# A two-column read of a shared PSUM bank, moved from a score block's fourth matmul to its fifteenth

## The chip, the cores and the metric
The program runs on one core of one Trainium2 chip. The metric is the device time of one execution in microseconds (us). Before the change the median of three runs is 3346.76 us (3344.51 to 3351.8).

## What the program computes
One transformer block over 1024 tokens of width 2048, plus 256 context tokens. Cut to the part that the change touches, the reference is a differential attention: every one of 8 heads has two maps, and their softmax weights are subtracted.

```
hx = modulate(rmsnorm(x), ...);  q, k, v, p, gb, gc, xin = split(hx @ w_in)      # k, v also from the context
s  = einsum('bqhmd,bkhmd->bhmqk', q, k) * 64 ** -0.5      # m = 0, 1: the two maps, 64 wide each
a  = softmax(s);  w = a[:, :, 0] - lam * a[:, :, 1];  o = w @ v
x  = x + gate * (concat(rmsnorm(o), pool_mix(p), conv_mix(gb, gc, xin)) @ w_out)
x  = x + gate2 * expert_choice_ffn(...);  return rmsnorm(x)
```

The whole is done in float32, where a product of two matrices is made of three matmuls on rounded high and low parts (high with high, high with low, low with high).

## The kernel before, in words
The program has four stages: modulation and projections for the first 768 tokens, the attention (with the projections of the other 256 tokens and a part of the output projection beside it), the rest of the output projection with norm and router, and the 16 experts.

The attention runs 64 steps: a head, a block of 256 queries, and one half of it (128 queries). Each step computes the scores of its 128 queries against 1280 keys for both maps. Python writes the steps one behind the other in a loop (functions `score`, `combine`, `turn`, `value`): the scores of the step two ahead, VectorE's combination of the next one's two exponentials, ten transposes of the combined weights in three groups (with casts to high and low parts by ACT and VectorE, tiles wth and wtl), and, for every second step, 30 matmuls of the weights with the values (tile av). Between them `fill` puts in a counted share of the projection matmuls (tile gm), whose weights ACT casts (line 439) and POOL completes (line 440). Small blocks for pooling and convolution run beside this (lines 847 to 904): a load of a tile pl_x or cv_z on SP's queue, a bias add on ACT (line 861, writes pl_x) or a scaling on ACT (line 896, writes e_out), and then POOL or VectorE.

What order the engines finally work in is not Python's alone. The tile scheduler takes this order, works out which instruction needs which other one, and writes a list for each engine by its own model of when an instruction is ready. Each engine then works through its own list in order.

One score block (`score`, line 952) is 18 matmuls into one PSUM tile sc of 128 by 2560, map 0 in the first 1280 columns and map 1 behind it. PSUM is divided into banks of 512 columns of this type. Map 0 uses rows 0 to 63 of TensorE and map 1 rows 64 to 127, so that a matmul of each may run side by side. Each map's keys are cut into three chunks (table CH), each chunk takes three matmuls, and PAIRED sorts the 18 so that the maps alternate:

```
CH = (((1024, 1280), (0, 512), (512, 1024)), ((256, 768), (768, 1280), (0, 256)))
```

Map 0's first chunk fills columns 1024 to 1279, which is the first half of the third bank. Map 1's last chunk fills columns 1280 to 1535, the second half of the same bank. The two must not be written by both maps at once, and a copy on ACT of two columns (to a tile named turned, which nothing reads) orders them: it reads what map 0's first chunk wrote, and the next matmul on the tile waits for it. In sorted order, the matmuls 1, 3 and 4 are map 0's first chunk, and 15, 17 and 18 are map 1's last one. Behind the block VectorE takes the negated maximum of each map (line 970, tile nm), and ACT the exponential with its sum (line 975, tile e). There is one tile sc, so a block can start only when the second exponential of the block before it has read it.

Of the kernel before, what the change touches and what calls it, by code (L numbers as in the profile page):

```python
# [9 lines left out]
F32 = mybir.dt.float32  # L10
# [10 lines left out]
P = 128  # L21
# [135 lines left out]
def nosync(tc, later, earlier):  # L157
    if earlier is not None:
        tc.add_manual_dep(later.ins, earlier.ins.name,
                          mybir.DependencyInfo(mybir.DependencyClass.NoSync, mybir.DependencyReason.DATA),  # L160
                          reason="accumulation groups of one bank in order")


def block_kernel(tc, I, out, dbg=None):
    nc = tc.nc
    pe, act, dve, gp, sp = nc.tensor, nc.scalar, nc.vector, nc.gpsimd, nc.sync
# [3 lines left out]
    def mm(o, l, r, start=True, stop=True):  # L170
        return pe.matmul(o, l, r, start=start, stop=stop, skip_group_check=True)  # L171
# [403 lines left out]
    def run_chunk(*args, beside=None):  # L575
        c = ChunkA(*args)
        for k in range(KT):
            if beside:
                next(beside, None)
            c.step(k)  # L580
        run_later()
        return c
# [67 lines left out]
    for h in range(HEADS):  # L650
        c = run_chunk(OFF_Q + h * P)
# [7 lines left out]
    for g in range(4):  # L659
        c = run_chunk(OFF_GC + g * P)  # L660
# [4 lines left out]
        c = run_chunk(OFF_X + g * P)  # L665
# [24 lines left out]
    sc = psc.tile([P, 2 * NKEY], F32, name="sc")  # L690
# [6 lines left out]
    asm = mk("asm", bufs=2, side="right")  # L697
# [257 lines left out]
    def score(i):  # L955
        h, b, qt = steps[i]
        q = Q_[h, b]
        k = K_[visit[i]]
        for _, m, c, n in PAIRED:
            c0, c1 = CH[m][c]  # L960
            rows = slice(64 * m, 64 * m + 64)
            one = mm(sc[:, m * NKEY + c0:m * NKEY + c1], q[rows, n // 2, qt * P:(qt + 1) * P], k[rows, n % 2, c0:c1],
               start=(n == 0), stop=(n == 2))
            if (m, c, n) == (0, 0, 2):
                act.copy(asm.tile([P, 2], F32, name="turned", tag="turned"), sc[:, c0:c0 + 2])
        scored.append(one)
        for m in range(2):
            s = sc[:, m * NKEY:(m + 1) * NKEY]
            nm = asm.tile([P, 1], F32, name="nm", tag=f"nm{m}")
            r = dve.tensor_reduce(nm, s, axis=AX, op=ALU.max, negate=True)  # L970
            if T["nsy"]:
                nosync(tc, r, last_stt[0])
            e = ep.tile([P, NKEY], F32, name=f"e{m}", tag=f"e{m}", bufs=(LEAD + 1, 2)[m])
            ssum = s0C[:, b, h, qt:qt + 1] if m == 0 else asm.tile([P, 1], F32, name="s1", tag="s1")
            act.activation(e, s, AF.Exp, bias=nm, scale=1.0, accum_out=ssum)  # L975
            E_[i, m] = (e, ssum)
# [195 lines left out]
    if True:  # L1172
# [14 lines left out]
        for i in range(LEAD):  # L1187
            score(i)
            fill(T["f3"])
# [3 lines left out]
        for i in range(NS):  # L1193
# [16 lines left out]
            for op in T[("late" if late else "even") if qt == 0 else ("lato" if late else "odd")]:  # L1210
                if isinstance(op, float):
                    part(op)
                elif op == "S" and nxt:
                    score(nxt)
                elif op == "V":
                    if waiting is not None:
                        value(waiting)
                        if visit[waiting] != visit[i]:
                            load_v(visit[i], 1)
                        waiting = None  # L1220
                    if i + 2 < NS and visit[i + 2] != visit[i]:
                        load_v(visit[i + 2], 0)
                elif op[0] == "T":
                    turn(i, int(op[1]))
                elif op == "C" and i + 1 < NS:
                    combine(i + 1)
# [436 lines left out]
```

## Time and profile before

| what | value |
|---|---|
| median of three runs | 3346.76 us |
| the profiled execution | 3349.19 us |
| its span, from the first to the last instruction | 3347.4 us |
| TensorE matmuls busy | 3070.2 us, 92% of the span |
| VectorE, ACT, POOL busy | 2258.2, 1768.6, 879.7 us |
| reads of sc into turned | 64, 10.7 us in all |

All rows are from one profiled execution. Times are counted from the start of its span. PE is TensorE's matmuls and PEld its weight loads, which overlap the matmuls; DVE is VectorE, POOL is GpSimd, SP the engine that issues most loads. L171 is the helper through which nearly every matmul is recorded, so matmuls are told apart by their tiles: `sc<-ks,qs` is a score matmul, `gm` a projection, `av` a value matmul, `trw` a transpose of weights. An arrow in brackets names what ended an engine's idle time. A row of the timeline with x4 merges four equal or like instructions that follow each other, with the time from the first's start to the last's end.

### The profile page before, as it was taken

To read this page: it belongs to the slowest core of one execution; us is meant where nothing else is said; L and a number is where in the kernel's file an instruction comes from. 1 tells how busy PE (TensorE), PEld (TensorE's weight loads), DVE (VectorE), ACT (ScalarE), POOL (GpSimd) and SP (SyncE) were. 2 spreads that over 40 slices of the span, in tenths; PEclk is the share of its full clock that TensorE was granted. 3 is DMA by queue.
4 is the path that set the end of the run, shared out by engine and by line. 5 is a ranking of instruction groups with operands and counts; after the bars stand their busy time and mean duration, and the time that the engine had idled before them with its cause. 6 is when DMAs were issued, how large, how long until landed. Compare 5 with 4: busy or idle time off the path is not lost. (4 is left out here: it accounts for less than half of the span.)

```text
span 3347.4 us, 48671 instructions
## 1 busy us (share of the span) xinstructions
PE 3070.2 (92%) x18783; PEld 2627.1 (78%) x18783; DVE 2258.2 (67%) x2744; ACT 1768.6 (53%) x2555; POOL 879.7 (26%) x581
## 2 busy tenths in 40 slices
PE   7999999999979889878999989699999999999995
PEld 4689989888868778777989878588777777777774
DVE  5235765662257766676555579788888888888877
ACT  5213322362245556554444344577766677676665
POOL 1001100010245555544667676220000000000021
PEclk9999999999989999999999999799999999999998
DMA  9965877633466555547787876899999999999998
GB/s 313 288 211 191 279 282 247 225 123 92 122 186 176 157 156 160 172 137 223 242 266 245 301 251 214 346 335 384 380 371 369 359 369 372 363 377 368 355 331 311
DMA packets 501851, 891.24 MB, mean 266 GB/s; under 512 B 24913, under 2 KB 356258, under 8 KB 490738
## 3 DMA queue, kind: packets, MB, share of 16 engines
q1 hardware_dynamic: 476960, 788.27, 67.2%
q0 software_dynamic: 24560, 99.83, 9.6%
q8 instruction: 147, 2.41, 0.3%
q14 instruction: 86, 0.70, 0.1%
q10 hardware_dynamic: 98, 0.03, 0.0%
HBM read 797.80 MB, written 90.23 MB: 265 GB/s over the span
## 5 line engine op out<-in xcount | busy, mean ns | idle before, releaser
L1443 DVE TENSOR_TENSOR es_t<-er_t,es_t 128x1024 fp32r<-128x1024 f32 x764 | 888.5, 1220 | 99.9 <-ACT es_t L1439 98.3
L1439 ACT CAST es_t<-er_t 128x1024 fp32r<-128x1024 f32 x768 | 775.8, 1052 | 181.0 <-PE gu L171 99.1
L440 POOL TENSOR_TENSOR w_split<-w_raw,w_split 128x1024 fp32r<-128x1024 f32 x208 | 547.1, 2636 | 441.3 <-ACT w_split L439 417.3
L171 PE MATMUL g_x<-hxh,w_split 128*128 128x512 f32 (+3 forms) x2560 | 592.5, 341 | 1.1 <-DVE w_split L440 1.1
L439 ACT CAST w_split<-w_raw 128x1024 fp32r<-128x1024 f32 x288 | 301.7, 1049 | 450.0 <-PE g_x L171 136.1
L171 PEld LDWEIGHTS g_x<-hxh,w_split 128*128 128x128 f32 x2560 | 396.7, 189 | 52.4 <-issue 9.9
L171 PE MATMUL gm<-w_split,mxh 128*128 128x256 f32 x2048 | 387.7, 289 | 11.3 <-DVE oy L1135 4.3
L171 PEld LDWEIGHTS gm<-w_split,mxh 128*128 128x128 f32 x2048 | 324.8, 194 | 17.6 <-issue 8.1
L171 PE MATMUL g_x<-hxl,w_split 128*128 128x256 f32 (+1 forms) x1280 | 331.6, 339 | 0.0
L171 PE MATMUL gu<-es_t,xh 128*128 128x512 f32 x1024 | 291.4, 405 | 22.5 <-DVE es_t L1443 22.5
L171 PE MATMUL dn<-es_t,hh 128*128 128x512 f32 x1024 | 300.0, 404 | 10.3 <-DVE es_t L1443 6.4
L171 PE MATMUL gm<-w_split,mxl 128*128 128x256 f32 x1024 | 293.9, 287 | 1.9 <-DMA mxl<-mixP 1.1
L171 PE MATMUL gg<-es_t,xh 128*128 128x512 f32 x1024 | 290.3, 400 | 1.1 <-ACT xh L1509 1.1
L171 PE MATMUL gm<-hbh,w_split 128*128 128x256 f32 x1280 | 272.8, 299 | 16.2 <-ACT e_raw L513 13.1
L970 DVE TENSOR_REDUCE nm<-sc 128x1 f32<-128x1280 f32 x128 | 190.6, 1489 | 130.2 <-ACT e L975 79.1
L975 ACT ACTIVATE e<-sc,nm 128x1280 f32<-128x1280 f32 x128 | 170.2, 1330 | 161.8 <-DVE nm L970 161.2
L171 PEld LDWEIGHTS gu<-es_t,xh 128*128 128x128 f32 x1024 | 195.1, 192 | 74.2 <-DVE es_t L1443 27.8
L171 PEld LDWEIGHTS dn<-es_t,hh 128*128 128x128 f32 x1024 | 189.6, 190 | 62.4 <-DVE es_t L1443 15.9
L1499 POOL DMA_INDIRECT xg<-h2S,idxT x16 | 23.2, 1448 | 818.9 <-PE tre L1507 738.1
L171 PEld LDWEIGHTS gm<-hbh,w_split 128*128 128x128 f32 x1280 | 214.4, 197 | 27.4 <-ACT e_raw L513 16.0
L171 PEld LDWEIGHTS gg<-es_t,xh 128*128 128x128 f32 x1024 | 190.7, 189 | 47.2 <-DVE es_t L1443 2.2
L171 PEld LDWEIGHTS g_x<-hxl,w_split 128*128 128x128 f32 x1280 | 198.2, 189 | 23.8 <-issue 3.3
(301 smaller groups left out, 5131.1 us busy)
## 6 DMA issues: line engine op xcount, KB each, us to landing
er_t<-in_w_gate SPq DMA_DIRECT2D x128, 1024.0 KB, 8.3
er_t<-in_w_down SPq DMA_DIRECT2D x128, 1024.0 KB, 8.8
er_t<-in_w_up SPq DMA_DIRECT2D x122, 1024.0 KB, 13.0
ada_w<-in_w_ada SPq DMA_DIRECT2D x192, 512.0 KB, 5.6
w_raw<-in_w_in SPq DMA_DIRECT2D x160, 512.0 KB, 4.7
w_raw<-in_w_out SPq DMA_DIRECT2D x128, 512.0 KB, 5.7
ks<-kS POOLq DMA_DIRECT2D x16, 1280.0 KB, 8.3
vh<-vS POOLq DMA_DIRECT2D x16, 640.0 KB, 5.5
```

Source lines behind the costliest of these rows:

```text
L171: return pe.matmul(o, l, r, start=start, stop=stop, skip_group_check=True)
L439: act.copy(s[:, 0], r)
L440: lo_eng.tensor_tensor(s[:, 1], r, raw(s[:, 0]), op=ALU.subtract)
L970: r = dve.tensor_reduce(nm, s, axis=AX, op=ALU.max, negate=True)
L975: act.activation(e, s, AF.Exp, bias=nm, scale=1.0, accum_out=ssum)
L1439: c = act.copy(s[:, 0], r)
L1443: lo = (gp if on_gp else dve).tensor_tensor(s[:, 1], r, raw(s[:, 0]), op=ALU.subtract)
L1499: ins = gp.indirect_dma_start(out=xg, out_offset=None, in_=h2S, in_offset=bass.IndirectOffsetOnAxis(ap=idxT[:, e:e + 1], axis=0))
```

## The change
The read is moved inside `score`. Before, it was written right behind the fourth matmul (map 0, chunk 0, its third matmul). Now it is written right ahead of the fifteenth (map 1, chunk 2, its first matmul). What it reads is the same two columns, 1024 and 1025.

```
         for _, m, c, n in PAIRED:
             c0, c1 = CH[m][c]
             rows = slice(64 * m, 64 * m + 64)
+            if (m, c, n) == (1, 2, 0):
+                act.copy(asm.tile([P, 2], F32, name="turned", tag="turned"), sc[:, 1024:1026])
             one = mm(sc[:, m * NKEY + c0:m * NKEY + c1], q[rows, n // 2, qt * P:(qt + 1) * P], k[rows, n % 2, c0:c1],
                start=(n == 0), stop=(n == 2))
-            if (m, c, n) == (0, 0, 2):
-                act.copy(asm.tile([P, 2], F32, name="turned", tag="turned"), sc[:, c0:c0 + 2])
```

Since the scheduler makes the engines' lists anew, other instructions move as well. On TensorE, the fifth score block (head 0, third block of queries, first half) stood like this, with no other work inside it; the brackets name the semaphores that an instruction waits for:

```order
L997 MATMUL trw<-cst,e_8321 128x128
L171 MATMUL sc<-ks,qs 128x256 [waits DMASW6_49,Activation_49]
L171 MATMUL sc<-ks,qs 128x512
L171 MATMUL sc<-ks,qs 128x256 x2
L171 MATMUL sc<-ks,qs 128x512 [waits Activation_49]
L171 MATMUL sc<-ks,qs 128x512 x9
L171 MATMUL sc<-ks,qs 128x256
L171 MATMUL sc<-ks,qs 128x512
L171 MATMUL sc<-ks,qs 128x256 x2
```

The same block on TensorE now:

```order
L997 MATMUL trw<-cst,e_8321 128x128
L171 MATMUL sc<-ks,qs 128x256 [waits DMASW6_49,Activation_49]
L171 MATMUL sc<-ks,qs 128x512
L171 MATMUL sc<-ks,qs 128x256 x2
L171 MATMUL sc<-ks,qs 128x512 x10
L171 MATMUL sc<-ks,qs 128x256 [waits Activation_49]
L171 MATMUL sc<-ks,qs 128x512
L171 MATMUL sc<-ks,qs 128x256 x2
```

The second wait for ACT has moved from the fifth matmul to the fifteenth, and nothing else of this block has.

On ACT, around the read of the eleventh score block, the list was this (the first row is the second exponential of the block before):

```order
L975 ACTIVATE e_9319,s_9320<-sc,nm 128x1280 [waits DVE_49]
L1000 CAST wth<-trw 128x4x128 [waits PE_49]
L500 ACTIVATE m_hl<-trp,colB 128x256 [waits DMAHW5_49,PE_49]
L500 ACTIVATE m_hl<-e_out 128x256 [waits DMAHW6_49]
L965 COPY turned<-sc 128x2 [waits PE_49]
L896 ACTIVATE e_out<-cv_z,colB 128x256 [waits DMAHW2_49,DVE_49]
L1000 CAST wth<-trw 128x2x128 [waits PE_49]
L439 CAST w_split<-w_raw 128x1024 [waits DMAHW4_49,PE_49]
L975 ACTIVATE e_9456,st<-sc,nm 128x1280 [waits DVE_49]
L861 ACTIVATE pl_x<-pl_x,lsm 128x264 [waits DMAHW4_49,Pool_49]
```

The same place on ACT now:

```order
L975 ACTIVATE e_9319,s_9320<-sc,nm 128x1280 [waits DVE_49]
L896 ACTIVATE e_out<-cv_z,colB 128x256 [waits DMAHW1_49,DVE_49]
L861 ACTIVATE pl_x<-pl_x,lsm 128x264 [waits DVE_49,DMAHW3_49,Activation_49,Pool_49]
L963 COPY turned<-sc 128x2 [waits PE_49]
L1000 CAST wth<-trw 128x4x128 [waits PE_49]
L439 CAST w_split<-w_raw 128x1024 [waits DMAHW6_49,PE_49]
L975 ACTIVATE e_9456,st<-sc,nm 128x1280 [waits DVE_49]
```

The scaling e_out and the bias add pl_x, which wait for loads (DMAHW), stood behind the read and now stand ahead of it; the casts wth and m_hl, which stood ahead, are elsewhere.

On TensorE, the thirteenth block had two transposes between its fourth and its fifth matmul:

```order
L171 MATMUL sc<-ks,qs 128x256 x2
L997 MATMUL trw<-cst,e_9315 128x128 [waits DVE_49,PE_49]
L997 MATMUL trw<-cst,e_9315 128x128
L171 MATMUL sc<-ks,qs 128x512 [waits Activation_49]
L171 MATMUL sc<-ks,qs 128x512 x9
L171 MATMUL sc<-ks,qs 128x256
```

Now it has four value matmuls and four transposes between its fourteenth and its fifteenth:

```order
L171 MATMUL sc<-ks,qs 128x512 x10
L171 MATMUL av<-wth,vl 128x256
L171 MATMUL av<-wth,vh 128x256
L171 MATMUL av<-wtl,vh 128x256
L171 MATMUL av<-wth,vl 128x256
L997 MATMUL trw<-cst,e_9456 128x128 [waits PE_49]
L997 MATMUL trw<-cst,e_9456 128x128 x3
L171 MATMUL sc<-ks,qs 128x256 [waits Activation_49]
```

Work that is ready is put where TensorE would wait, and the place of that wait has moved by ten matmuls.

## Rows read from the trace of the kernel before

**Rows 1.** Stretch; busy us (count) of PE, PEld, DVE, ACT, POOL; clock; DMA.
```profile
930.00:1490.00 560.00, 480.61 (x3605) 428.06 (x3606) 388.16 (x541) 317.86 (x652) 284.34 (x213) 0.95 0.55 162
1490.00:1830.00 340.00, 313.25 (x2484) 295.22 (x2483) 193.70 (x272) 171.42 (x291) 210.24 (x115) 0.96 0.75 237
```
**Rows 2.** Reads of the tile turned by stretch: ACT busy us (instructions).
```profile
930.00:1490.00 560.00, 7.67 (x45) 0.95 0.55 162
1490.00:1830.00 340.00, 3.02 (x19) 0.96 0.75 237
```
**Rows 3.** Waits of TensorE, 930 to 1490: total us, times, longest.
```profile
PE sc L171 <- ACT turned L965: 19.8, 28, 3.7
PE sc L171 <- ACT e L975: 18.8, 18, 6.7
```
**Rows 4.** Waits of TensorE, 1490 to 1830.
```profile
PE trw L997 <- ACT turned L965: 2.7, 2, 2.3
```
**Rows 5.** Timeline of TensorE, third score block: start, us, what [idle before].
```profile
956.05 0.62 PE L171 MATMUL sc<-ks,qs 64*128 64x256 f32 x4 [0.16 <-ACT e L975]
956.92 1.78 PE L171 MATMUL sc<-ks,qs 64*128 64x512 f32 x14 [0.25 <-ACT turned L965]
```
**Rows 6.** Timeline of ACT, the third block's read.
```profile
956.70 0.16 ACT L965 COPY turned<-sc 128x2 f32<-128x2 f32 x1
```
**Rows 7.** Timeline of TensorE, fifth score block.
```profile
980.96 0.62 PE L171 MATMUL sc<-ks,qs 64*128 64x256 f32 x4
983.01 1.79 PE L171 MATMUL sc<-ks,qs 64*128 64x512 f32 x14 [1.44 <-ACT turned L965]
```
**Rows 8.** Timeline of ACT in the fifth block.
```profile
980.80 1.03 ACT L439 CAST w_split<-w_raw 128x1024 fp32r<-128x1024 f32 x1
981.73 0.41 ACT L500 ACTIVATE e_hl<-e_raw 128x256 fp32r<-128x256 f32 x1
982.05 0.85 ACT L1000 CAST wth<-trw 128x512 fp32r<-128x512 f32 x2
982.78 0.18 ACT L965 COPY turned<-sc 128x2 f32<-128x2 f32 x1
```
**Rows 9.** The tile turned: ns min/median/max, first and last start.
```profile
L965 ACT COPY turned<-sc x64: 141/160/214, 935.6 to 1813.1; 128x2 f32<-128x2 f32 x64
```
**Rows 10.** Timeline of TensorE, third block, matmuls five to fourteen alone.
```profile
956.92 1.43 PE L171 MATMUL sc<-ks,qs 64*128 64x512 f32 x10 [0.25 <-ACT turned L965]
```
**Rows 11.** Timeline of ACT, first score block.
```profile
935.16 0.51 ACT L896 ACTIVATE e_out<-cv_z,colB 128x256 f32<-128x256 f32 x1 [9.42 <-DMA cv_z<-zS]
```
**Rows 12.** Timeline of TensorE, first score block.
```profile
931.06 0.97 PE L171 MATMUL sc<-ks,qs 64*128 64x256 f32 x4 [5.11 <-DMA ks<-kS]
935.77 3.14 PE L171 MATMUL sc<-ks,qs 64*128 64x512 f32 x14 [3.74 <-ACT turned L965]
```
**Rows 13.** Timeline of TensorE, value matmuls, nine apart.
```profile
1206.19 0.28 PE L171 MATMUL av<-wth,vl 128*128 128x256 f32 x1
...
1207.26 0.28 PE L171 MATMUL av<-wth,vl 128*128 128x256 f32 x1
```
**Rows 14.** Waits of ACT, 930 to 1490: total us, times, longest.
```profile
ACT pl_x L861 <- DMA pl_x<-pS: 30.6, 11, 6.5
...
ACT e_out L896 <- DMA cv_z<-zS: 20.6, 6, 9.4
ACT e_out L896 <- DVE m_hl L502: 11.4, 5, 2.8
...
ACT e_out L896 <- POOL pl_y L868: 5.1, 2, 3.7
...
ACT turned L965 <- PE sc L171: 3.3, 2, 2.2
```
**Rows 15.** The tile pl_x: ns min/median/max; then the load's landing.
```profile
L861 ACT ACTIVATE pl_x<-pl_x,lsm x16: 284/516/522, 910.6 to 1399.7; 128x264 f32<-128x264 f32 x8, 128x272 f32<-128x272 f32 x4, 128x8 f32<-128x8 f32 x4
...
DMA to landing us min/median/max: 2.3/4.2/7.4
```
**Rows 16.** Line 896 on ACT, the scaling e_out.
```profile
L896 ACT ACTIVATE e_out<-cv_z,colB x16: 496/509/512, 911.0 to 1403.5; 128x256 f32<-128x256 f32 x16
```

More of the change, by code (lines that the diff above doesn't have):

```diff
@@ L961, in score @@
             rows = slice(64 * m, 64 * m + 64)
+            if (m, c, n) == (1, 2, 0):
+                act.copy(asm.tile([P, 2], F32, name="turned", tag="turned"), sc[:, 1024:1026])
             one = mm(sc[:, m * NKEY + c0:m * NKEY + c1], q[rows, n // 2, qt * P:(qt + 1) * P], k[rows, n % 2, c0:c1],
                start=(n == 0), stop=(n == 2))
-            if (m, c, n) == (0, 0, 2):
-                act.copy(asm.tile([P, 2], F32, name="turned", tag="turned"), sc[:, c0:c0 + 2])
         scored.append(one)
```

## The prediction
> **What bounds the kernel now.** The stages come first, from the table of busy time by stretch [rows 1]. The change touches only the attention stage, where 64 score blocks stand: 930 to 1490 us holds 45 of them, mixed with projection work, and 1490 to 1830 us the last 19, mixed mostly with the output projection [rows 2]. TensorE is busy 480.6 of 560 us in the first stretch and 313.3 of 340 us in the second. Nothing else is fuller (VectorE 388.2, ACT 317.9 of 560), so TensorE's order and its idle 79 us and 27 us decide there. Next the list of waits of TensorE over the first stretch [rows 3]: the largest of them is the score matmuls waiting for ACT's small read, 19.8 us in 28 waits, and the second is the first score matmul of a block waiting for the exponential that frees the score tile, 18.8 us in 18 waits. In the second stretch the read costs a transpose 2.7 us in two waits [rows 4]. So the read stands behind 22.5 us of idle TensorE; that is 0.67% of the program, and the most that the change can take away directly.
>
> Last the blocks one by one. The third block shows the bare hand-over [rows 5]: four matmuls from 956.05 us take 0.62 us to their end, the read starts 956.70 [rows 6] and takes 0.16, and the fifth matmul starts 956.92 after 0.25 us idle. The fifth block shows the costly form [rows 7]: the four matmuls are done at 981.58, but the fifth starts at 983.01, 1.44 us idle, because ACT, which takes its work in order, still had the weight cast (1.03 us), a small one (0.41) and two casts of transposed weights (0.85) to do ahead of the read, which starts at 982.78 [rows 8]. The mean wait is 19.8 / 28 = 0.7 us, so more than half of it is ACT being late, not the hand-over. How the new place changes this lateness is the question.
>
> **The change part by part.** Nothing is added or removed: 64 reads of 0.16 us before and after [rows 9], and as many matmuls. In the built program the read's wait counts every score matmul written ahead of it, so it now waits for the fourteenth of a block instead of the fourth, and TensorE's wait moves from the fifth to the fifteenth. The overlap inside a block is therefore not larger: the hand-over stays one full trip from TensorE to ACT and back. What changes is that ten matmuls now run first. In the third block these ten end 1.43 us after they start [rows 10]; about 1.3 us of that passes before another matmul could start (an estimate, less the overlap of the last one). So ACT has 1.3 us more in which to finish what stands ahead of the read.
>
> Term A, the stalls that go. The fifth block has the same four ACT casts ahead of its read in the new order. Four matmuls plus ten from 980.96 end at about 982.9, and ACT is free at 982.78, so 1.44 us becomes the bare 0.25. The first block is a special case: its read waits behind a scaling on ACT that itself waited 9.42 us for a load [rows 11], TensorE idles 3.74 us, and TensorE is slow there (fourteen matmuls take 3.14 us instead of 1.78) [rows 12]. Ten fourteenths of 3.14, 2.2 us, go under the wait, and 1.5 us stay. In the new order 58 of the 64 blocks have other TensorE work between the fourteenth and the fifteenth matmul (50 of 64 had some between the fourth and the fifth), mostly 2 to 6 transposes or 20 to 22 value matmuls. A value matmul takes 0.12 us from start to start, (1207.26 - 1206.19) / 9 [rows 13], so two or more cover the bare 0.25. Six blocks have none, the first among them; the other five keep 0.25 each, 1.25 us. A = 22.5 - 1.5 - 1.25 = 19.7 us.
>
> Term B, what the scheduler now puts ahead of the read. The tile scheduler writes each engine's order as its own model finds instructions ready; a later read leaves room ahead of it. In eight blocks ten ACT instructions that wait for loads have moved from behind the read to ahead of it: six pl_x bias adds and four e_out scalings. While they wait, the read waits, and with it the fifteenth matmul. In the trace of before, where they mostly stood behind the read, pl_x waited 30.6 us for its load and e_out 20.6 us for loads, 11.4 us for VectorE and 5.1 us for POOL [rows 14]. There are 16 of each [rows 15, 16], so pl_x costs 30.6 / 16 = 1.9 us, and e_out, without the first block's 9.4, 27.7 / 16 = 1.7 us. Ten of them come to 6 x 1.9 + 4 x 1.7 = 18 us with no cover, which is the upper bound by these means; the lower bound is zero, when the load is there in time. The cover is 1.3 us of matmuls in each block plus the inserted work: 22 value matmuls (2.6 us) in two blocks, 5 to 8 small ones (about 0.7 us) in six, so 3.9 and 2.0 us. Only the two blocks with two such instructions, at 3.6 and 3.8 us, exceed it: 1.6 + 1.8 = 3.4 us. I take 3.4, by the means; since single pl_x waits reached 6.5 us, the 18 stays as an end for the range.
>
> What else the move holds up. ACT may now reach the read before TensorE does, and then all that is queued behind it waits: the block's own exponential, which needs the block anyway, and casts of transposed weights, which only work inserted at that same place needs soon. In before ACT idled for the read 3.3 us in all [rows 14]. If 1.3 us more fell in each of the 17 blocks of the first stretch where TensorE did not wait, ACT would lose 22 us, hidden by its 242 us of idle time there; I cost it at nothing. DMA issues on SP and POOL are reordered by the scheduler, with no count changed; I have no row that prices this and leave it to the range.
>
> How much comes back. A - B = 16.3 us of TensorE time. Of 45 block starts in the first stretch, 18 waited for the exponential [rows 3]; there the loop of scores, maximum and exponential sets the pace, and TensorE finishing early may only wait longer at the next start. I count the remaining 27 of 45: 16.3 x 0.6 = 9.8 us. The profiled execution took 3349.2 us, 1.8 above its span of 3347.4; by it the changed kernel would take 3339.4. The median of the three timed runs is 3346.8, 2.4 below, and the forecast stands against that one: 3337 us.
>
> A rule bears on the last step. TensorE's weight loads are busy 428.1 of the 560 us, its matmuls 480.6 [rows 1]. The Trainium skill, page "Perfetto Trace Analysis", section "Identifying the Most-Contended Engine", holds that matmul busy time is a poor measure of how near TensorE is to its limit, and that the busy share of weight loads is the better one. By it the headroom is 132 us and not 79, TensorE is less the bound, and less than 0.6 comes back: it leans towards the first rival. The list of waits speaks against it, since the largest single idle cause is the read itself.
>
> **The rivals.** First, the idle time comes back elsewhere: the blocks finish earlier, but the next start waits for the exponential. For it: 18.8 us of such waits already [rows 3]. Against it: those waits would have to grow by nearly all of A, and 27 of 45 starts do not wait for it at all. Time: about 3347. Second, the stall only moves: ACT gets as much ahead of the read as it gained time, and the mean of 0.7 us stays at the fifteenth matmul. For it: the hand-over itself is the same and the scheduler does fill ACT's gap. Against it: 58 covered blocks. Time: 3347 as well. Third, on the other side, slower: the loads decide. The ten moved instructions wait in ACT's queue for data, each block's last four matmuls stand behind them, and the maximum and exponential behind those. At the longest waits shown (6.5 for each pl_x, 3.7 for each e_out [rows 14]) they would cost 39 + 15 = 54 us, less the cover of 2 x 3.9 + 6 x 2.0 = 20, so 34; 34 x 0.6 is 20, less 19.7 x 0.6 = 12 of A: some 9 us slower, 3356. It decides once the mean wait of the ten exceeds (20 + 19.7) / 10 = 4.0 us, twice the mean of before. Against it: a pl_x load lands 4.2 us after its issue at the median [rows 15], while the blocks stand 13.9 us apart, (1813.1 - 935.6) / 63 [rows 9].
>
> **How the numbers follow.** Forecast 0.50, first rival 0.20, second 0.10, third 0.20. A measurement of this kernel can tell 0.2%, 6.7 us, from no change, so faster means below 3340.1 and slower above 3353.5. The forecast is the faster case, the first two rivals are the same case, the third the slower one: 0.50, 0.30, 0.20. The likeliest case by itself lies between 3327 (all of A, nothing of B, all of it back) and 3340. The range for 8 in 10 adds room of 2 us at the fast end for reordered queues, 3325, and at the slow end takes in both middle rivals and the third up to just past its worked-out 3356, to 3357; some 1 in 10 is left out on either side.
>
> **What would show it.** In the changed profile the waits of score matmuls for the read should fall from 19.8 to 3 to 8 us, and TensorE's idle time between 930 and 1490 from 79 to about 63, with the last score block some 10 us earlier. The waits for the exponential should grow by no more than 6 us; if they take up the whole drop, the first rival holds. If the read's waits stay at some 20 us behind ordinary casts, the second does. If pl_x or e_out rows stand directly ahead of long waits of the fifteenth matmul, term B was too small. A difference outside 930 to 1830 us would be none of this and would make the whole argument wrong.

## The result and the profile after

The changed kernel takes 3369.82 us (median of five runs, 3367.47 to 3384.18) beside 3350.97 us for the kernel before in the same comparison (3344.51 to 3354.44): a ratio of 1.0070, 95% interval 1.0054 to 1.0086. The ratio is estimated from all these runs; the two medians by themselves lie 18.9 us apart, 0.56%. The changed kernel is slower by 0.7%, where 3337 us was forecast and 3357 us was the end of the range. The profiled run took 3367.47 us with a span of 3365.7.

The busy times of the two attention stretches, in the columns of [rows 1]:

```profile
930.00:1490.00 560.00, 470.64 (x3459) 417.25 (x3457) 375.29 (x526) 312.49 (x634) 263.28 (x206) 0.94 0.52 154
1490.00:1830.00 340.00, 315.62 (x2455) 294.68 (x2453) 202.49 (x271) 169.97 (x287) 205.55 (x110) 0.95 0.70 226
```

TensorE is less busy than before in the first stretch, by 10 us, and did 146 matmuls fewer there. To compare like with like one has to cut by work and not by time. From the start of the third score block to the end of the last one TensorE runs 5929 matmuls in both kernels. The same view of that stretch, of the kernel before and then of the changed one:

```profile
955.80:1818.90 863.10, 768.32 (x5929) 701.04 (x5928) 562.48 (x787) 471.04 (x915) 479.00 (x314) 0.96 0.62 189
```
```profile
951.10:1840.80 889.70, 781.96 (x5929) 709.58 (x5930) 569.84 (x788) 478.13 (x916) 469.42 (x314) 0.95 0.59 183
```

The third block starts 4.7 us earlier than before, and the last one ends 21.9 us later. In between, 26.6 us were lost: 13.6 as busy time (781.96 - 768.32, the same matmuls at a granted clock of 0.95 and not 0.96) and 13.0 as idle time (107.7 against 94.8, each stretch less its busy time). The span grew by 18.3, so 3.6 us came back behind the attention.

Where the idle time sits is read from TensorE's waits between 930 and 1490 us, which answer to [rows 3]; total us, times, longest:

```profile
PE trw L997 <- DVE wtl L1001: 35.8, 23, 4.3
PE sc L171 <- ACT e L975: 16.8, 15, 4.6
PE sc L171 <- ACT turned L963: 12.1, 10, 3.3
```

The stall at the read fell from 19.8 us in 28 waits to 12.1 in 10, and the waits for the exponential fell a little too. A new row leads the list: transposes of weights wait 35.8 us for wtl, VectorE's subtraction that gives their bank back. In the kernel before that row was 7.8 us:

```profile
PE trw L997 <- DVE wtl L1001: 7.8, 11, 1.8
```

These 560 us hold less work in the changed kernel. Over the two windows of equal work the same rows say it more sharply: the waits for wtl rose from 10.3 to 39.7 us, those at the read fell from 15.8 to 11.9 and those for the exponential from 21.9 to 12.9.

VectorE in turn waits longer for TensorE. The two rows of its waits in the same stretch, before and then after:

```profile
DVE nm L970 <- PE sc L171: 15.2, 19, 2.3
DVE at L1016 <- PE av L171: 4.6, 7, 1.7
```
```profile
DVE nm L970 <- PE sc L171: 25.2, 14, 4.3
DVE at L1016 <- PE av L171: 17.5, 12, 2.6
```

The row maximum nm waits for the last matmuls of a block, and `at`, VectorE's step that takes a finished group of 30 value matmuls out of PSUM, for the last of them. ACT's waits, as in [rows 14]:

```profile
ACT turned L963 <- PE sc L171: 46.1, 28, 4.5
ACT pl_x L861 <- DMA pl_x<-pS: 42.8, 12, 7.9
...
ACT e_out L896 <- DMA cv_z<-zS: 15.2, 4, 9.2
```

ACT is held at the read for 46.1 us (3.3 before), and its waits for these two loads are 58.0 us in all (51.2 before). Six of the ten waits at the read stand behind an ACT instruction that had waited for a load. In the first block it cost the bare 0.25 us; in blocks 11, 13, 15, 25 and 34 a pl_x stands directly ahead of the read, and their stalls are 1.55, 0.30, 3.25, 3.07 and 1.75 us, 9.9 of the 12.1. Two places show both sides of the change. The fifth block on TensorE, which answers to [rows 7]:

```profile
979.32 0.62 PE L171 MATMUL sc<-ks,qs 64*128 64x256 f32 x4 [0.25 <-ACT turned L963]
```

Its 1.44 us of stall became 0.25. The eleventh block, TensorE first, then ACT, then VectorE:

```profile
1054.91 0.28 PE L171 MATMUL av<-wth,vh 128*128 128x256 f32 x1
1055.12 1.78 PE L171 MATMUL sc<-ks,qs 64*128 64x256 f32 x14
1056.83 0.39 PE L171 MATMUL av<-wtl,vh 128*128 128x256 f32 x1
1057.17 0.60 PE L997 MATMUL trw<-cst,e 128*128 128x128 f32 x4
1059.32 0.62 PE L171 MATMUL sc<-ks,qs 64*128 64x256 f32 x4 [1.55 <-ACT turned L963]
```
```profile
1058.71 0.51 ACT L861 ACTIVATE pl_x<-pl_x,lsm 128x264 f32<-128x264 f32 x1 [5.07 <-DMA pl_x<-pS]
1059.13 0.14 ACT L963 COPY turned<-sc 128x2 f32<-128x2 f32 x1
1059.17 0.59 ACT L1000 CAST wth<-trw 128x512 fp32r<-128x512 f32 x1
```
```profile
1057.46 0.41 DVE L1016 TENSOR_SCALAR at<-av 128x256 f32<-128x256 f32 x1
1060.05 1.49 DVE L970 TENSOR_REDUCE nm<-sc 128x1 f32<-128x1280 f32 x1 [2.17 <-PE sc L171]
1061.45 0.68 DVE L1001 TENSOR_TENSOR wtl<-trw,wth 128x512 fp32r<-128x512 f32 x1
```

Of a group of 30 value matmuls, 28 ran ahead of the block (the last at 1054.91), and the other two were listed into the wait (the first at 1056.83), with four transposes. Behind them the last four score matmuls still waited 1.55 us, for a read behind a pl_x that waited 5.07 us for its load. The row maximum came late, and wtl, which frees the bank of the four transposes, stood behind it: 1061.45, 3.7 us after those transposes had ended. The first 2.0 us of these are ACT's: wtl needs the cast wth, which stood behind the read and ended at 1059.76. The value group did not delay wtl by way of `at`, which was done at 1057.87.

In the whole attention 27 of the 32 value groups now stand around a score block; before it was 13, and most of the others ran through in 3.75 to 4.8 us. The 23 waits for wtl can be followed back through VectorE's work as long as it had no gap. In 11 of them (18.3 us) a row maximum stands ahead of the late wtl, in five (5.6 us) wtl itself waited for ACT's cast, and in only two (3.4 us) an `at` stands ahead of it, one of them in a chain that begins with a row maximum.

### The profile page after: what moved, and what is told of

It reads as the page before. It is cut to its first block, busy times and chain, and to the rows that moved or that the text cites. A ratio compares the mean times of both kernels' runs of the same rounds, so it can differ in the third digit from the quotient of the medians.

```text
span 3365.7 us, 48697 instructions
## 1 busy us (share of the span) xinstructions
PE 3088.1 (92%) x18783; PEld 2639.6 (78%) x18783; DVE 2260.9 (67%) x2744; ACT 1775.4 (53%) x2555; POOL 872.0 (26%) x581
## 5 line engine op out<-in xcount | busy, mean ns | idle before, releaser
L440 POOL TENSOR_TENSOR w_split<-w_raw,w_split 128x1024 fp32r<-128x1024 f32 x208 | 539.2, 2600 | 396.8 <-ACT w_split L439 390.3
L171 PE MATMUL gm<-hbh,w_split 128*128 128x256 f32 x1280 | 269.5, 301 | 16.3 <-ACT e_raw L513 13.6
```

Source lines behind the costliest of these rows:

```text
L440: lo_eng.tensor_tensor(s[:, 1], r, raw(s[:, 0]), op=ALU.subtract)
```

## The experiments

Three theories stood at the start. A: work listed into the wait of the late read, transposes above all, meets banks that VectorE has not given back and holds the last four matmuls. B: pl_x and e_out, which wait for loads, stand ahead of the read on ACT. C: ACT, held at the late read, is late with the casts behind it. Beside them there is the chance that a newly written list alone moves the time.

All times are medians, with the ratio to the kernel before in the same comparison. "Late" is the changed kernel's place of the read, "early" that of the kernel before. The ratio is estimated from all runs of both kernels in that comparison, and the median of the kernel before lies between 3348.81 and 3354.92 us in them, so small differences are better read from the ratios than from the medians. Counts of what stands inside a block are from the built programs.

| run | read | edit | us | ratio, 95% interval |
|---|---|---|---|---|
| e1 | late | transposes and value matmuls held back | 3350.34 | 0.9998 (0.9986, 1.0010) |
| e2 | early | the same | 3366.70 | 1.0067 (1.0041, 1.0092) |
| e6 | late | transposes held back | 3364.24 | 1.0033 (1.0017, 1.0048) |
| e11 | late | value matmuls held back | 3340.90 | 0.9974 (0.9960, 0.9989) |
| e18 | early | the same | 3351.83 | 0.9996 (0.9980, 1.0011) |
| e3 | late | pl_x, e_out behind the read, step later | 3332.26 | 0.9939 (0.9920, 0.9957) |
| e5 | early | the same | 3331.56 | 0.9936 (0.9913, 0.9958) |
| e9 | late | pl_x, e_out behind the read | 3333.28 | 0.9943 (0.9925, 0.9961) |
| e12 | late | loads two blocks ahead, on SyncE | 3372.47 | 1.0078 (1.0058, 1.0099) |
| e13 | early | the same | 3359.26 | 1.0034 (1.0019, 1.0049) |
| e14 | late | loads two blocks ahead, on ScalarE | 3372.18 | 1.0053 (1.0037, 1.0070) |
| e15 | early | the same | 3367.35 | 1.0045 (1.0029, 1.0061) |
| e16 | late | read by VectorE | 3375.35 | 1.0072 (1.0055, 1.0089) |
| e17 | early | the same | 3376.67 | 1.0066 (1.0050, 1.0083) |
| e8 | 9th | read ahead of the ninth matmul | 3358.64 | 1.0018 (1.0004, 1.0031) |
| e10 | 12th | read ahead of the twelfth | 3379.31 | 1.0088 (1.0063, 1.0112) |
| e4 | early | only the fifteenth waits for it | 3334.36 | 0.9950 (0.9934, 0.9966) |
| e7 | early | e4 with e5's edits | 3298.26 | 0.9848 (0.9815, 0.9881) |

**Work listed into the wait: e1, e2, e6, e11, e18.** `nosync(tc, later, earlier)` keeps the first instruction behind the second in the engine's list and adds no wait. e1 and e2 carry both edits, e6 the first, e11 and e18 the second:

```
-            pe.transpose(t[:, (k - a) * P:(k - a + 1) * P], e0[...], ident)
+            nosync(tc, pe.transpose(t[:, (k - a) * P:(k - a + 1) * P], e0[...], ident), scored[-1])
...
-                    mm(o, vv[:, k, :], ww, start=(n == 0), stop=(n == 29))
+                    nosync(tc, mm(o, vv[:, k, :], ww, start=(n == 0), stop=(n == 29)), scored[-1])
```

> The changed kernel with the step's transposes and value matmuls ordered behind the newest score block's last matmul, so that they cannot stand between its fourteenth and fifteenth. Theory A (transposes placed in the wait meet a PSUM bank that VectorE's wtl has not freed, and hold the last four matmuls behind them): the waits of trw for wtl fall from some 40 us to 10 to 15, and the time to 3335 to 3355. Theory B (loads that pl_x and e_out wait for stand ahead of the read): no help, 3362 to 3375. Theory C (ACT is held at the read, 46 us in the stretch, and its casts come late): no help, 3362 to 3375, with ACT still waiting over 35 us at the read.

> The control for the one above: the kernel before with the same ordering of transposes and value matmuls. Theory A: the place of the read hardly matters once nothing is pulled into the wait, so this and the pinned changed kernel lie within 8 us of each other. Theories B and C: this one stays 12 to 25 us faster than the pinned changed kernel.

With both kinds held back the late read is no longer slower than the kernel before (0.9998), and against its own control, e2, it is 16 us faster. But e2 itself is 15 us slower than the kernel before in its comparison, and theory A wanted the two within 8 us of each other; holding work back is not free. So the next runs held back one kind each.

> The changed kernel, in which only the attention's transposes of weights (trw) may not be listed ahead of the newest block's last score; the value matmuls may. 54 of the 640 transposes are then still listed inside a block, against 181 in the changed kernel, and 389 value matmuls, against 400. Theory A (it is the transposes: their bank is given back by VectorE's subtraction, which stands behind the row maxima): waits of trw for wtl fall from 35.8 us to under 15 us between 930 and 1490 us, and the time to 3340-3356 us. If the value matmuls listed in the wait cost as much as the transposes: 3358-3370 us. Theory B (loads ahead of the read): 22 pl_x and 20 e_out still stand ahead of it, so the wait of scores for the read stays at 10-20 us, and the time moves by less than 6 us, 3362-3372 us.

> The changed kernel in which only the value matmuls (av) may not be listed ahead of the newest block's last score; 138 transposes still are (changed kernel 181; with both held back 72, with the transposes alone held back 54). With both held back the time was 3350 us, with the transposes alone 3364 us. Theory A: waits of trw for wtl of 20-36 us between 930 and 1490 us, and 3358-3370 us. If it is the value matmuls, which take the engine from the scores while VectorE and ScalarE wait for the next block: waits of trw for wtl no matter, 3346-3356 us.

> The kernel before, its value matmuls not listed ahead of the newest block's last score; 115 transposes still are inside a block (before 111), and no value matmul (before 265). It is the control of e11 (late read, values held back: 3341 us). If the value matmuls in the wait are the late read's loss, the early read has little to gain from holding them back: 3346-3366 us, so that the late read is the faster of the two, as first predicted, by 5 us or more. If holding them back is faster in itself wherever the read is: 3318-3338 us, and the late read loses as before.

TensorE's waits between 930 and 1490 us in e6:

```profile
PE sc L171 <- ACT e L975: 29.4, 19, 5.1
PE trw L997 <- DVE wtl L1001: 15.9, 12, 2.9
```

In e6 the waits for wtl fell as theory A wanted, and a large part came back as waits for the exponential (16.8 to 29.4). By the medians 6 us of 19 returned, by the ratios about half (1.0033 beside 1.0070). So the transposes alone do not carry the loss. In e11, TensorE's waits and then two rows of VectorE's:

```profile
PE sc L171 <- ACT turned L963: 20.8, 24, 3.0
...
PE trw L997 <- DVE wtl L1001: 12.2, 8, 3.9
```
```profile
DVE nm L970 <- PE sc L171: 9.4, 10, 2.2
DVE at L1016 <- PE av L171: 9.0, 7, 3.1
```

With 138 transposes still inside a block but no value matmul, the waits for wtl fell from 35.8 to 12.2, the row maximum's wait for the block from 25.2 to 9.4, and the time by 29 us. The stall at the read is larger than in the changed kernel (20.8 against 12.1), so the value matmuls do cover part of it; the time says that the cover cost more than it hid. The time is below the range that either theory gave. The control e18 does not move (0.9996). So with value matmuls held back the late read is no slower than the early one: 0.9974 against 0.9996 is 7 us faster by the ratios (the two intervals overlap, so a gain is not shown; the 11 us between the two medians come in part from two comparisons whose kernel before differs by 4). With the value matmuls free it is slower by 19 to 23.

**Loads and ScalarE's list: e3, e5, e9, e12 to e15.** e9 has the first edit alone, e3 and e5 the second as well:

```
-        act.activation(biased, biased, AF.Identity, bias=bias_pg[:, g:g + 1])
+        nosync(tc, act.activation(biased, biased, AF.Identity, bias=bias_pg[:, g:g + 1]), last_read[0])   # e_out alike
...
-            next_block()
+            (called behind score(nxt) in the same step)
```

> The changed kernel with the pooling and convolution blocks started after the score block, and their first ACT instruction (pl_x, e_out) ordered behind the read. Theory B: the read's waits on TensorE fall from 12 to under 4 us and the time comes back by half or more, 3348 to 3360. Theories A and C: trw still waits over 30 us for wtl, ACT over 35 us at the read, and the time stays at 3362 to 3375.

> The kernel before, its read behind the fourth matmul as it was, with the two edits of the run 'blocks behind the read': the next block's load-and-filter step is issued behind the scores, and ScalarE's pl_x and e_out of a block are ordered behind the newest read. It is the control of that run (3332 us, 37 us under the changed kernel). Theory B (loads that stand ahead of the read on ScalarE hold the matmul that waits for the read; at the late place this costs some 10 us, at the early one some 20): the wait of scores for the read falls from 19.8 us to under 12 us between 930 and 1490 us, and the time to 3335-3347 us. If the gain comes from the blocks' later place alone, whatever the place of the read: 3326-3336 us, as with the late read. Theory A (the transposes listed in the wait of the late read come too early for VectorE) says nothing for this kernel, since its read is early: 3345-3356 us. Re-listing alone: no bound, and no wait that explains it.

> The changed kernel with one of the two edits of the run 'blocks behind the read' alone: ScalarE's pl_x and e_out of a block are ordered behind the newest read; the block's step is issued where it was. 14 pl_x and 15 e_out then stand ahead of a read (changed kernel 25 and 24), but 232 of the 640 transposes are listed inside a block, the most of all these kernels (changed kernel 181), and 27 groups of them have their wtl behind that block's first row maximum on VectorE (21; before 1). Theory A (the transposes listed in the wait of the late read cost by the banks that VectorE gives back late): waits of trw for wtl of 36 us or more between 930 and 1490 us, and 3366-3382 us. Theory B (ScalarE's loads, waited for in front of the read and of the casts behind it): as the run with both edits, 3326-3342 us, with waits of trw for wtl under 20 us, since wtl is late because ScalarE is.

All three are 0.6% faster than the kernel before, and late and early no longer differ. e3 is faster than any theory had it. e5 came out where it was expected if the later place of the blocks pays by itself, wherever the read is. e9 has the time that theory B expected, and the wait for wtl nearly so (21.0 us, expected under 20). TensorE's waits in e5, then in e9, and one of ACT's in e9:

```profile
PE sc L171 <- ACT e L976: 13.5, 18, 4.0
PE sc L171 <- ACT turned L966: 13.3, 23, 1.6
PE trw L998 <- DVE wtl L1002: 10.6, 12, 1.7
```

```profile
PE trw L998 <- DVE wtl L1002: 21.0, 20, 3.5
...
PE sc L171 <- ACT turned L964: 0.5, 2, 0.2
```
```profile
ACT turned L964 <- PE sc L171: 76.1, 42, 4.9
```

In e9 232 transposes are inside a block, more than in any other kernel; the waits for wtl still fell to 21.0. That speaks against theory A in its first form. The stall at the read is gone (0.5 us), while in e5 it is 13.3 us, and yet both take the same time: here a stall removed brought nothing. e12 to e15 asked whether it is the late loads themselves:

```
-    plc=2,  plx=2,
+    plc=3,  plx=3,
...
-            loaded.pop()()
-        if blocks:
+            loaded.pop(0)()
+        while blocks and len(loaded) < 2:
...
```

In e14 and e15 the blocks' four `sp.dma_start` became `act.dma_start` as well.

> The changed kernel with the loads of the filter blocks issued one step earlier: two blocks are loaded ahead instead of one, with three buffers instead of two for pl_x and cv_z and for their second operands. The listing stays nearly the changed kernel's: 23 pl_x and 25 e_out stand ahead of a read (25 and 24), 174 transposes and 392 value matmuls are listed inside a block (181 and 400). If the loss is ScalarE standing for late loads: pl_x and e_out wait under 10 us for loads between 930 and 1490 us (changed kernel 58), and the time falls to that of the runs with the loads' instructions behind the read, 3326-3345 us. If it is the listing: no row of loads' waits left, and still 3355-3375 us.

> The same early loads in the kernel before, the read behind the fourth matmul. With the loads out of the way the two places of the read differed by under 2 us in the runs with pl_x and e_out behind the read (3332 and 3333 against 3332). If late loads are what the late place suffers from: this kernel and the one with the late read within 6 us of each other, both 3326-3345 us. If it is the listing: this kernel faster than the one with the late read by 12-25 us. If the moved read brings what was predicted once the loads are there: this one slower by some 10 us.

> The kernel of e12 (changed kernel, loads two blocks ahead, three buffers) with the loads of the filter blocks issued by ScalarE instead of SyncE. 20 pl_x and 19 e_out stand ahead of a read (changed kernel 25 and 24), 190 transposes and 421 value matmuls are listed inside a block (181 and 400). If the loss is ScalarE standing for late loads: its waits for loads of pl_x and cv_z under 12 us between 930 and 1490 us (changed kernel 58.0), and 3326-3345 us. If it is the listing around the read: those waits gone and still 3358-3376 us. The issues themselves cost ScalarE 64 instructions, beside its idle time.

> The same loads from ScalarE's queue in the kernel before, the read behind the fourth matmul. If late loads are what the late place suffers from: within 6 us of the kernel with the late read and the same loads, both 3326-3345 us. If it is the listing: 12-25 us faster than that one. If the moved read brings what was predicted once the loads are there: some 10 us slower than that one.

ACT's waits for the loads in e12, then in e14:

```profile
ACT pl_x L861 <- DMA pl_x<-pS: 52.9, 11, 11.3
ACT e_out L896 <- DMA cv_z<-zS: 4.8, 4, 2.7
```
```profile
ACT pl_x L861 <- DMA pl_x<-pS: 37.7, 11, 7.5
...
ACT turned L964 <- DMA cv_z<-zS: 4.8, 1, 4.8
ACT turned L964 <- DVE at L1017: 4.3, 1, 4.3
...
ACT e_out L896 <- DMA cv_z<-zS: 2.1, 2, 1.6
```

In e12 the edit failed: 57.7 us in all, as in the changed kernel. In e14 the two waits are 39.8 us, 18 us fewer, and the time stayed at 3372. But ACT, which now issues the loads, stands at new waits ahead of the read, 4.8 and 4.3 us of them in the rows shown, so about half of what went came back in the same place. The bound that was set (under 12 us) was not reached either. The test is weak. The early reads, e13 and e15, are 13 and 5 us faster than their late ones, and neither came near 3345 us. That leans to the side of the listing; but both are slower than the kernel before, by 0.3 and 0.4%, and e15 is as near to e14 as late loads would have it.

**ScalarE held at the read: e16, e17.** `act.copy` became `dve.tensor_copy` at either place.

> The changed kernel with the read, at the same place, done by VectorE instead of ScalarE. 216 transposes and 382 value matmuls are listed inside a block (changed kernel 181 and 400); ScalarE has no read any more. Behind the read on VectorE stand mostly the subtractions wtl that give back the transposes' banks. If the loss came from ScalarE held at the read (46 us between 930 and 1490 us in the changed kernel) with its casts behind: 3328-3350 us. If it is the work listed in the wait: 3362-3380 us, and trw still waits for wtl for 30 us or more. If an engine held at the read loses whichever it is: over 3372 us, since VectorE is the fuller one (375 against 312 us of 560).

> The control of the run before it: the kernel before with its early read done by VectorE. 144 transposes and 282 value matmuls inside a block. VectorE's queue stands ahead of the read, row maxima of 1.5 us and combinations of 1.6 us among it, so the wait of the scores for the read may grow: 3345-3375 us. If ScalarE held at the late read is the loss, the late one is the faster of the two, by 10 us or more; if the work listed in the wait is, the early one is, by 10 us or more.

TensorE's waits in e16:

```profile
PE trw L997 <- DVE wtl L1001: 37.1, 24, 4.1
...
PE sc L171 <- DVE turned L963: 10.2, 11, 3.1
```

ACT has no read any more, and the list of waits and the time are those of the changed kernel. The time fits the third expectation too, that any engine held at the read loses; but VectorE waits for the scores there for only 15.4 us in all, and e9, where ACT is held longest, is fast. So theory C, a loss by the hold itself, falls on e9; e16 alone would not settle it, since there VectorE, which makes the wtl, is held instead. The control e17 is as slow as e16, where a difference of 10 us was expected either way, so the pair says nothing on the place itself.

**The place in between: e8, e10.** The copy stands ahead of matmul nine or twelve.

> The kernel before with the read ahead of the ninth matmul, halfway to the changed kernel's place (ahead of the fifteenth). Other work is listed at the wait in 56 blocks (before 50, changed kernel 58), 157 of 640 transposes among it (before 111, changed 181). Theory A: waits of trw for wtl of 18-32 us between 930 and 1490 us (before 7.8, changed 35.8), time 3354-3370 us. Theory B (loads ahead of the read hold the matmul that waits, and cost the less cover the read has): the same place relative to the loads as in the changed kernel, 3345-3358 us. Re-listing alone: the time is not between before and changed, or the waits don't follow it.

> The kernel before with the read ahead of the twelfth matmul: the series is the fifth (before, 3351-3354 us), the ninth (3359), the fifteenth (changed kernel, 3370). Other work at the wait in 60 blocks, 184 transposes, 335 value matmuls, 26 pl_x and 24 e_out ahead of reads: as in the changed kernel. If the listing counts (theories A and B, both settled by what stands around the read): as the changed kernel, 3364-3378 us. If the place itself counts, by the matmuls that cover the read or by ScalarE's time in the wait: between the ninth and the fifteenth, 3358-3368 us. Re-listing alone: outside 3355-3378 us.

3351, 3359, 3379, 3370 us for the fifth, ninth, twelfth and fifteenth matmul: every later place is slower, but not in order. The waits of trw for wtl are 17.0 us in e8 and 16.8 in e10, so they do not set e10, the slowest, apart; there the read (17.2) and the projections' waits for e_raw (16.4, before 9.6) are as large. e10 lies just outside what either the listing or the place had allowed (up to 3378), where it was expected for re-listing alone. Part of the series is the listing of each kernel and not the place.

**An early read that nothing but the fifteenth waits for: e4, e7.** The matmuls 5 to 14 write other banks than the one that is read:

```
+            if read is not None and at < 14:
+                tc.declare_no_dep(one.ins, read.ins, reason="other banks than the read's")
             if (m, c, n) == (0, 0, 2):
-                act.copy(...
+                read = act.copy(...
```

> The read is written behind the fourth matmul as before, but matmuls five to fourteen, which write other banks, no longer wait for it; the fifteenth does. Theory C: ACT is not held longer than before (under 10 us at the read) and TensorE has ten matmuls to cover the hand-over, so the read's waits on TensorE fall under 6 us and the time is 3330 to 3347, faster than before. Theory A: other work is still put ahead of the fifteenth matmul in 48 blocks, so trw waits over 25 us for wtl and the time is 3352 to 3368. Theory B: as before or faster, since no more loads stand ahead of the read than before, 3340 to 3352.

> The two edits that were faster, together: the read behind the fourth matmul as in the kernel before, but only the fifteenth waits for it, and a block's load-and-filter step issued behind the scores, with its pl_x and e_out behind the newest read on ScalarE. If the two take away different waits (3334 and 3332 us alone): 3312-3328 us, with under 4 us of scores' waits for the read between 930 and 1490 us. If they take away the same one (what B says of the loads is also what a read with ten matmuls to spare no longer feels): 3326-3338 us. Re-listing alone: anywhere from 3325 to 3355 us.

TensorE's waits in e4:

```profile
PE trw L1000 <- DVE wtl L1004: 11.1, 11, 2.8
...
PE sc L171 <- ACT turned L968: 4.7, 6, 2.1
```

This is what the change was expected to do: the stall at the read falls by 15 us and some 17 come back (0.5%). The read can be done while ten matmuls run. The scheduler still lists other work in front of the fifteenth in 48 blocks, but less of it: 198 value matmuls, fewer than before (265, in front of the fifth) and half as many as in the changed kernel (400). Theory A's forecast, over 25 us of waits for wtl and 3352 us or more, failed; theory C's time came out. Since ACT's hold and the listed work both shrank, e4 does not tell the two apart. With e5's edits it is the best version, 3298 us, 1.5% faster than before, 2.1% faster than the changed kernel and below the range expected. From e5 to e7 the edit alone brought 33 us, more than on its own and more than any re-listing moved.

## Why the prediction was wrong

**What was right.** The difference lies in the attention: 21.9 us at its end, of which 3.6 came back behind it. The overlap of ten more matmuls is real: the fifth block came out to the hundredth (1.44 to 0.25), and the first block took 4.4 us from its first matmul to its end where it had taken 7.8, a gain of 3.5 us for a forecast of 2.2. (The third block starts 4.7 us earlier; 2.7 of these were there before the first block began.)

**The step that failed: the cover in term A.** "In the new order 58 of the 64 blocks have other TensorE work between the fourteenth and the fifteenth matmul ... A value matmul takes 0.12 us from start to start, so two or more cover the bare 0.25." That took inserted work as free cover. It stands in front of the block's last four matmuls, and with them of the row maximum, the exponential and the next block. Measured: trw's waits for wtl +28.0 us, while the stall at the read gave 7.7. With the value matmuls held back the late read took 3341 us and not 3370, and lost nothing against the early read held back alike (e18); with both kinds held back the loss went too (e1, 0.9998). That is the evidence that the loss goes with the listing of the value matmuls, as long as the loads' instructions stay ahead of the read. It does not show the forecast gain of 9.8 us, since the 7 us between e11 and e18 are not clear of their intervals.

By which wait the listed work costs its time is not shown. A path by way of `at`, held back by the split value groups, is not borne out: only two of the 23 late wtl have an `at` ahead of them, and in e16, as slow as the changed kernel, VectorE's `at` waits 8.8 us, in the fast e11 9.0. The row maximum stands ahead of more of them, but the number of value matmuls inside blocks does not order the times either: e3 has 361 at 3332 us, e8 390 at 3359, e10 335 at 3379.

**Term B was too small.** 3.4 us were taken beyond the cover. Measured were 9.9 us of stalls behind a pl_x that had itself waited for its load or stood behind an e_out that had. The bound of 18 held.

**"What else the move holds up", at nothing.** ACT's hold is twice what was worked out (46.1 against 22 us). In e9 a longer hold, 76.1 us, goes with a fast kernel, so the hold by itself is not where the time went.

**The share that comes back, 0.6.** It has no fixed value: about all of it in e4, none between e5 and e3, where waits for the exponential (13.5 to 23.3) and for wtl (10.6 to 17.9) took the place of the stall.

**The signs and the rivals.** The read's waits came to 12.1 us (3 to 8 were named), TensorE's idle time between 930 and 1490 us to 89.4, the stretch less 470.64 (63), and the last block was late and not early. The sign for term B, pl_x rows directly ahead of long waits, came true. The first and second rival fall: the waits for the exponential fell, the stall shrank, and the time did not stay. The third had the sign but not the sum: the stalls behind loads had to exceed the 19.7 us of A and came to 9.9. That the loads cost their time by another path, through the casts that stand behind them on ACT, is not excluded: e9 behaves as that would have it, and e14 is too weak to speak against it.

**The size.** 13.6 of the 26.6 us is busy time of the same matmuls at a lower granted clock, which no term had.

**What stays open.** Listing pl_x and e_out behind the read takes the loss away too (e3, e9 against e5), with 361 and 295 value matmuls still inside a block. That this and the value matmuls are one chain, since ACT's late casts and VectorE's late subtractions work on the same transposes, is argued and not shown. Edits that should have done little at the early place moved the time by up to 24 us (e2, e13, e15, e17), as much as the change itself, so a pair that differs by less settles nothing alone. The 29 us of e11 against the changed kernel, borne out by e1 (0.9998 beside 1.0070), go beyond that; the 17 us of e4 alone do not, the 33 from e5 to e7 do. A kernel without the ordering read was not tried.

## What to carry to other kernels

A wait that is moved later is a hole that the scheduler fills, and what it puts there stands in front of everything behind the wait: look at which groups are split around it, whose buffers they hold and what waits behind them. Rather than moving a small ordering instruction towards its consumer, leave it early and narrow down who waits for it (e4, and more clearly e7 against e5). Compare two lists by the same work and not the same time, and build a control at the old place for each edit, since re-listing alone can be worth as much as the change.

## What was not expected of the hardware

The same 5929 matmuls were busy 13.6 us longer. In the three stretches of the changed kernel below, the clock falls after TensorE had been waiting; the granted clock is third from the end of the row:

```profile
1547.40:1557.40 10.00, 10.00 (x83) 9.61 (x82) 4.87 (x5) 5.10 (x11) 3.08 (x2) 1.00 0.32 92
1557.40:1567.40 10.00, 7.19 (x59) 6.23 (x57) 8.05 (x12) 5.63 (x10) 4.69 (x3) 1.00 0.45 131
1567.40:1581.00 13.60, 10.26 (x44) 8.62 (x45) 11.72 (x19) 5.53 (x14) 6.63 (x4) 0.51 0.98 315
```

TensorE was busy all of the first 10 us and 7.19 of the next 10, at 2.4 GHz; then 13.6 us were granted at 0.51, which is the level of 1.2 GHz, and 44 matmuls took 10.26 us of busy time. Idle time of TensorE is here paid partly twice, once as such and once in the clock behind it. In the fastest version, e7, the same work has 64.2 us of idle time and 7.9 us less busy time than the kernel before:

```profile
942.70:1767.40 824.70, 760.46 (x5929) 698.96 (x5928) 563.32 (x793) 475.95 (x920) 481.81 (x323) 0.97 0.65 199
```
